# A decoder layer in split fp32: three operand splits of the second MLP product, and the sums of the first norm, moved in the hand-written order

## The chip, the cores and the metric

One core of a Trainium2 chip runs one launch of the whole step. The metric is device time in microseconds (us), the median of the runs shown. The engines are PE (TensorE, matmuls), DVE (VectorE), ACT (ScalarE), POOL (GpSimd) and SP (SyncE, which here only issues DMAs).

## What is computed

One inference step of a one-layer hybrid decoder over 1104 tokens (16 meta, 1024 prompt, 64 new ones), D_MODEL 1024, D_FF 4096. Cut to what the change touches:

```python
u = _rmsnorm(h, norm_mix)
z = u @ w_in + b_in                 # pooling, conv, q, k, v and gates come out of z
...
h = h + merged.astype(h.dtype) @ w_out
u2 = _rmsnorm(h, norm_mlp)
h = h + jnp.square(jax.nn.relu(u2 @ w_up)) @ w_down
```

## The kernel before, in words

**Numbers.** Every fp32 operand of a product is split into a high part (ACT writes it, `hi = Copy(x)`) and a low part (DVE writes it, `lo = x - hi`), and three matmuls, hi·hi, hi·lo and lo·hi, make one product. A split is therefore one ACT and one DVE instruction, in `split` (L155 to L157) for activations and in `Weights.split_to` (L93, L94) for weights. In `split_to` the DVE half is put off until `flush`, and the raw weight comes by a DMA (L64) into one of two buffers.

**Order.** The whole program runs under a manual schedule: each engine takes its instructions in the order in which the code issues them, and waits where an operand or a buffer is not ready. `slot()` issues the DMA stores put off so far, and takes steps from a list.

**Head.** The first five tiles of `w_in` (NHEAD) meet the tokens in three chunks of 416, 320 and 368 (CH). `proj_mm(ti, ci)` is the product of weight tile `ti` with chunk `ci` on PE, 24 matmuls, into a PSUM bank; `proj_chunk` reads that bank on DVE (`un`, L903, times the norm factor `rb`) and ACT. PSUM has three banks called `pm` and two called `pn` for these products, taken in turn, so that product (0,1), tile 0 with chunk 1, writes the bank in which product (0,0) stood, and has to wait for its `un`. `norm1(ci)` is the norm of chunk 1 or 2 as a list of steps: steps 0 and 1 square the chunk on ACT and add it up on DVE (`sq`, L304, L306); step 2 (`s1`) sums over the partitions on PE (L260), makes the factor on DVE and ACT (L246 to L251) and spreads it into three diagonal blocks on DVE (`diag`, L266); step 3 (`s2`) multiplies these with ones on PE, which broadcasts the factor (`px`, L271). In the code `n1` is chunk 1 and `n2` chunk 2, so `n1[2]` is the sum of chunk 1 and `n2[3]` the broadcast of chunk 2.

**First MLP product.** Sixteen pairs of tiles of `w_up` (NPAIR), each by seven block products (`product`, a Strassen-Winograd scheme), i = 0 to 6. Product 6 adds onto the bank of products 0, 2 and 4, so it must wait until DVE has read product 4 out of it (`cb`, L1614). `op_steps` squares the result and makes the seven combinations that the second product takes; they go to memory (`opB..`, `opT..`).

**Second MLP product.** Seven products n = 0 to 6, each of four row pairs `mp` with two half-products `hf` of 48 matmuls (`dprod`); half-product 0 takes the operand pages 0 to 3, half-product 1 the pages 4 to 7. An operand page (n, q) is loaded by `op_load` (L1547, tile `ld`, one of five `page2` buffers) and split by `op_split` into `oph` and `opl`. Pages 0 to 6 of product n = 0 are loaded and split beside the seven products of the last pair; page 7 comes straight from the last steps, without memory. The weights of half-products 1 and 2 are loaded (`W.load_to(3)`) beside product 4 of the last pair. In the split loop and in `dprod`'s loop the order is what is written there, nothing else.

Of the kernel before, what the change touches and what calls it, by code (L numbers as in the profile page):

```python
# [114 lines left out]
def hybrid_trunk_kernel(ctx, tc, I, O):  # L115
# [16 lines left out]
    def pmain():  # L132
        W.tick()
        if wide:
            wide[0] += 1
            if wide[0] % 5 > 2:
                return psum.tile([P, 512], F32, name="pn", tag="qk", bufs=2)
        return psum.tile([P, 512], F32, name="pm", tag="pm", bufs=3)
# [9 lines left out]
    def mm3(ps, wh, wl, pairs, first=True, last=True):  # L148
        n = len(pairs)
        for i, (k, (xh, xl)) in enumerate(pairs):  # L150
            PE.matmul(ps, lhsT=wh[k], rhs=xh, start=first and i == 0, stop=False)  # L151
            PE.matmul(ps, lhsT=wh[k], rhs=xl, start=False, stop=False)  # L152
            PE.matmul(ps, lhsT=wl[k], rhs=xh, start=False, stop=last and i == n - 1)  # L153
# [689 lines left out]
    def sview(t, off, n):  # L843
        return t[:, off:off + 8 * n].rearrange("p (s t) -> p s t", s=8)
# [34 lines left out]
    def proj_mm(ti, ci):  # L879
        kind, j = TILES[ti]  # L880
        wh, wl = wts[ti][:2]
        a, c = CH[ci]
        if kind in "qz" and ci == 0:
            a = NM
        ps = pmain()
        mm3(ps[:, :c - a], wh, wl, [(k, (Uh[k][:, a:c], Ul[k][:, a:c])) for k in range(8)])
        return ps

    def proj_chunk(ti, ci, ps=None):
        kind, j = TILES[ti]  # L890
        t = wts[ti][2]
        if ps is None:
            ps = proj_mm(ti, ci)
        e, es = t.get("e"), t.get("s")
        b = bin_[:, ti:ti + 1]
        a, c = CH[ci]
        if kind in "qz" and ci == 0:
            a = NM
        w = c - a
        pp = min(c, S0) - a  # L900
        if ci < 2 and ti < NHEAD:
            un = apool.tile([P, 416], F32, name="un", tag="zs", bufs=2)
            V.tensor_tensor(un[:, :w], ps[:, :w], rb[:, a:c], ALU.mult)  # L903
            ps = un
        if kind == "g":
            A.activation(sig[j - 4][:, a:c], ps[:, :w], AF.Identity if ti < NHEAD else AF.Sigmoid,
                         bias=b)
        elif kind == "c" and ti < NHEAD:
            A.activation(e[:, 14 + a:14 + a + pp], ps[:, :pp], AF.Identity, bias=b)
            if ci == 2:  # L910
                A.activation(es[:, :, 30:], sview(ps, pp, 8), AF.Identity, bias=b)
        elif kind == "c":
            V.scalar_tensor_tensor(e[:, 14 + a:14 + a + pp], ps[:, :pp], b,
                                   sig[j][:, a:a + pp], ALU.add, ALU.mult)
            if ci == 2:
                V.scalar_tensor_tensor(es[:, :, 30:], sview(ps, pp, 8), b,
                                       sview(sig[j], S0, 8), ALU.add, ALU.mult)
        elif kind == "a":
            A.activation(e[:, a:a + pp], ps[:, :pp], AF.Identity, bias=b)
            if ci == 2:  # L920
                A.activation(es[:, :, 15:], sview(ps, pp, 8), AF.Identity, bias=b)
        elif kind in "kv":
            A.activation(e[:, a:c], ps[:, :w], AF.Identity, bias=b)
        elif kind == "q":
            A.activation(e[:, a - NM:c - NM], ps[:, :w], AF.Identity, bias=b)
        else:
            z = apool.tile([P, 416], F32, name="zs", tag="zs", bufs=2)
            A.activation(z[:, :w], ps[:, :w], AF.Identity, bias=b)
            store(gD[j][:, a - NM:c - NM], z[:, :w])
# [136 lines left out]
    b0_ = [proj_mm(0, 0)]  # L1066
# [27 lines left out]
    n2 = norm1(2)  # L1094
    proj_open(4)
    b0_.append(proj_mm(4, 0))
    n1[2]()
    n2[0]()
    n2[1]()
    proj_chunk(3, 0, b0_[3])  # L1100
    b1_ = [proj_mm(0, 1)]
    proj_chunk(4, 0, b0_[4])
    b1_.append(proj_mm(1, 1))
    n1[3]()
    n2[2]()
    b1_.append(proj_mm(2, 1))
    proj_chunk(0, 1, b1_[0])
    proj_chunk(1, 1, b1_[1])
    n2[3]()
# [434 lines left out]
    def op_load(n, q):  # L1544
        if n < NPROD:
            ld[n, q] = page2("ld")
            SP.dma_start(ld[n, q][:, :L], opD[DORD[n][1], q])  # L1547

    def op_split(n, q):
        if n < NPROD:  # L1550
            t = ld.pop((n, q))
            h, l = BD[n, q] = page("oph", F32R), page("opl", F32R)
            split(h[:, :L], l[:, :L], t[:, :L])
# [27 lines left out]
    for s in range(7 * NPAIR):  # L1581
        j, i = divmod(s, 7)
        if j and i < 4:
            steps[i]()
        if i == 0:
            sums = down_sums(j)
        if i in sums:
            sums[i]()
        if i == 0:
            ca, cb, s15, u2 = page("ca"), page("cb"), page("s15"), page("u2")  # L1590
            bk = [wide_tile(), None, None]
        elif i == 1:
            bk[1] = wide_tile()
        elif i == 5:
            bk[2] = wide_tile()
        if s + 3 < 7 * NPAIR:
            prep(s + 3)
        if j == NPAIR - 1 and i == 0:
            W.load_to(1)
            op_load(0, 0)  # L1600
            op_load(0, 1)
        if j + 1 < NPAIR and 2 <= i < 6:
            sum_pair(j + 1, i - 2)
        product(bk[(0, 1, 0, 1, 0, 2, 0)[i]], s, i, i in (0, 1, 5))
        if i == 0:
            A.activation(two(s15), view(bk[0]), AF.Copy)
        elif i == 1:
            A.activation(two(s15, HL), view(bk[1]), AF.Copy)
        elif i == 2:
            A.activation(two(u2), view(bk[0]), AF.Copy)  # L1610
        elif i == 3:
            V.tensor_tensor(two(ca, HL), view(bk[1]), two(u2), ALU.add)
        elif i == 4:
            V.tensor_tensor(two(cb, HL), view(bk[0]), two(s15, HL), ALU.add)  # L1614
            if j + 2 < NPAIR:
                load_pair(j + 2)
        elif i == 5:
            V.tensor_tensor(two(ca), view(bk[2]), two(s15), ALU.add)
        else:
            A.activation(two(cb), view(bk[0]), AF.Copy)  # L1620
            square(ca)
            steps = op_steps(j, ca, cb)
        if j == NPAIR - 1:
            for n in range(2):
                BC.pop((BX[i], n))
            if i < 5:
                op_split(0, i)
                op_load(0, i + 2)
            elif i == 5:
                op_split(0, 5)  # L1630
                op_split(0, 6)
                op_load(1, 0)
                op_load(1, 1)
            if i == 1:
                W.split_to(1)
                W.flush()
            elif i == 4:
                W.load_to(3)
            elif i == 5:
                W.split_to(2)  # L1640
                W.flush()
        slot()
# [134 lines left out]
    for n in range(NPROD - 1):  # L1777
        for mp in range(4):
            if n == 0:
                H[2 * mp], H[2 * mp + 1] = page("h"), page("h")  # L1780
            b = wide_tile()
            for hf in range(2):
                i = 8 * n + 2 * mp + hf
                WD[n, mp, hf] = W.get(i)
                W.split_to(i + 2)
                W.flush()
                q = 2 * mp + hf
                op_split(n + 1, q)
                if q < 6:
                    op_load(n + 1, q + 2)  # L1790
                elif n + 2 < NPROD:
                    op_load(n + 2, q - 6)
                if 3 <= n < 6 and hf:
                    if n != 5:
                        residual_load(2 * mp + (n == 3), HI)
                    if n != 3:
                        residual_load(2 * mp + (n == 5), LO)
                if n == NPROD - 2 and q == 7:
                    W.load_to(i + 4)
                dprod(n, mp, hf, b, TWO)  # L1800
                WD.pop((n, mp, hf))
                slot(3 if n == 4 and hf == 0 else 1)
            evict(n, mp, b)
            if n == 3:
                attq.extend(done(2 * mp + 1, HI))
            elif n == 4:
                attq.extend(done(2 * mp, HI))
                attq.append(lambda m=2 * mp: residual(m, LO))
            elif n == 5:
                attq.append(lambda m=2 * mp + 1: residual(m, LO))  # L1810


    n = NPROD - 1
# [4 lines left out]
    for e, (a, c) in enumerate(ENDS):  # L1818
        w = c - a
        q = None  # L1820
        for mp in range(4):
            b = wide_tile()
            for hf in range(2):
                i = 8 * n + 2 * mp + hf
# [11 lines left out]
            q = page("fsq")  # L1836
# [139 lines left out]
```

## Time and profile before

| | us |
|---|---|
| median of 3 runs (1661.28 to 1661.79) | 1661.78 |
| the profiled execution, its own time | 1662.0 |
| its span, first to last instruction | 1660.1 |
| PE busy in it (99% of the span) | 1642.7 |
| DVE busy (68%) | 1134.5 |
| ACT busy (45%) | 750.5 |

The span is what the trace covers; 1.9 us of the execution's own time lie around it. PE is busy nearly all the time, so a row matters where PE waits, where it runs at the lower of its two clocks, and where another engine's queue decides when PE may go on. In a timeline row the first number is the start in us from the span's start, the second the length from the first start to the last end of the merged instructions; `[idle before <-releaser]` stands behind a row before which its engine waited. Matmuls overlap, so a matmul's length is more than the distance to the next.

### The profile page before, as it was taken

The numbers are of one execution on the slowest core, as the hardware profiler recorded it, in microseconds if no ns is written. First come the engines' busy times: TensorE is split into PE (matmuls) and PEld (weight loads), VectorE is DVE, ScalarE is ACT, GpSimd is POOL, SyncE is SP. The second block draws the span as 40 slices with busy tenths as digits, with TensorE's granted clock in tenths as the row PEclk, the third lists the DMA queues.
The fourth block names the chain that finished last, engine by engine and source line by source line (L and its number), as shares of the span: only waits on it lengthen the run. The fifth ranks groups of instructions, "written<-read, shape, count | busy, mean of one in ns | idle before, by whom it ended". The sixth has DMA issues, their size and how long they took to land.

```text
span 1660.1 us, 28943 instructions
## 1 busy us (share of the span) xinstructions
PE 1642.7 (99%) x11568; PEld 1618.2 (97%) x11568; DVE 1134.5 (68%) x2120; ACT 750.5 (45%) x1428; POOL 5.8 (0%) x14
## 2 busy tenths in 40 slices
PE   9999999999999999999999999999999999999997
PEld 8999999999999999999999999999999999999997
DVE  7786767867776666455584687777777844457674
ACT  6537667467675342364243343233332533333341
POOL 0000000000000000000000000000000000000000
PEclk9999999999999999999999999999999999999998
DMA  6051221231225353344253447777776955556652
GB/s 207 15 110 52 71 79 42 68 77 41 81 63 173 97 197 113 104 184 146 80 172 124 152 162 242 244 237 246 243 241 227 323 194 184 183 184 222 204 173 85
DMA packets 132123, 250.78 MB, mean 151 GB/s; under 512 B 33459, under 2 KB 64148, under 8 KB 131988
## 3 DMA queue, kind: packets, MB, share of 16 engines
q1 hardware_dynamic: 131428, 248.45, 46.2%
q8 instruction: 91, 1.49, 0.4%
q10 hardware_dynamic: 560, 0.48, 0.1%
q14 instruction: 44, 0.36, 0.1%
HBM read 168.52 MB, written 80.36 MB: 150 GB/s over the span
## 4 chain that ended last, share of the span: by engine, by line
PE 95%; DVE 2%; ACT 1%; DMA 1%; issue 0%; SPq 0%; DVEq 0%; ACTq 0%
PE pm L151 13%; PE pm L153 13%; PE pm L152 13%; PE m L1663 7%; PE m L1665 7%; PE m L1667 7%; PE m L1470 6%; PE m L1473 6%; PE m L1472 6%; PE pn L151 3%; PE pn L153 3%; PE pn L152 3%; PE px L634 2%; PE px L622 2%; PE qk L581 2%; PE px L271 1%
## 5 line engine op out<-in xcount | busy, mean ns | idle before, releaser
L151 PE MATMUL pm<-uh,whi 128*128 128x320 f32 (+3 forms) x1008 | 338.5, 336 | 0.6 <-ACT uh L342 0.5
L153 PE MATMUL pm<-uh,wlo 128*128 128x320 f32 (+3 forms) x1008 | 333.1, 330 | 0.0
L152 PE MATMUL pm<-ul,whi 128*128 128x320 f32 (+3 forms) x1008 | 332.2, 330 | 0.6 <-DVE ul L343 0.6
L1663 PE MATMUL m<-oph,whi 128*128 128x272 f32 (+2 forms) x896 | 258.5, 289 | 0.0
L1665 PE MATMUL m<-opl,whi 128*128 128x272 f32 (+2 forms) x896 | 258.0, 288 | 0.0
L1667 PE MATMUL m<-oph,wlo 128*128 128x272 f32 (+2 forms) x896 | 257.8, 288 | 0.0
L93 ACT ACTIVATE whi<-wraw 128x1024 fp32r<-128x1024 f32 (+1 forms) x127 | 130.0, 1025 | 205.6 <-PE m L1665 138.3
L94 DVE TENSOR_TENSOR wlo<-wraw,whi 128x1024 fp32r<-128x1024 f32 (+1 forms) x127 | 150.6, 1187 | 98.3 <-ACT whi L93 98.3
L151 PEld LDWEIGHTS pm<-uh,whi 128*128 128x128 f32 x1008 | 190.8, 189 | 2.6 <-ACT uh L342 1.3
L152 PEld LDWEIGHTS pm<-ul,whi 128*128 128x128 f32 x1008 | 191.3, 190 | 1.9 <-DVE ul L343 1.5
L153 PEld LDWEIGHTS pm<-uh,wlo 128*128 128x128 f32 x1008 | 190.3, 189 | 0.4
L1665 PEld LDWEIGHTS m<-opl,whi 128*128 128x128 f32 x896 | 168.8, 188 | 0.0
L1663 PEld LDWEIGHTS m<-oph,whi 128*128 128x128 f32 x896 | 168.6, 188 | 0.0
L1667 PEld LDWEIGHTS m<-oph,wlo 128*128 128x128 f32 x896 | 168.5, 188 | 0.0
L456 DVE SCALAR_TENSOR_TENSOR y<-ext,vec,y 128x1024 f32<-128x1024 f32 x120 | 152.5, 1271 | 0.0
L1470 PE MATMUL m<-bch,wlo 128*128 128x272 f32 x448 | 129.2, 288 | 2.0 <-DVE cb L1614 2.0
L1470 PE MATMUL m<-bch,whi 128*128 128x272 f32 x448 | 129.3, 289 | 0.6 <-DVE h L1409 0.6
L1473 PE MATMUL m<-bch,whi 128*128 128x272 f32 x448 | 128.9, 288 | 0.0
L1473 PE MATMUL m<-bch,wlo 128*128 128x272 f32 x448 | 128.8, 288 | 0.0
L1472 PE MATMUL m<-bcl,whi 128*128 128x272 f32 x448 | 128.7, 287 | 0.0
L1472 PE MATMUL m<-bcl,wlo 128*128 128x272 f32 x448 | 128.7, 287 | 0.0
L1470 PEld LDWEIGHTS m<-bch,wlo 128*128 128x128 f32 x448 | 84.2, 188 | 2.2 <-issue 2.2
(364 smaller groups left out, 3418.1 us busy)
## 6 DMA issues: line engine op xcount, KB each, us to landing
wraw<-w_in SPq DMA_DIRECT2D x46, 512.0 KB, 3.9
opT<-d SPq DMA_DIRECT2D x64, 272.0 KB, 3.0
ld<-opT SPq DMA_DIRECT2D x32, 544.0 KB, 4.6
wd<-w_down SPq DMA_DIRECT2D x32, 512.0 KB, 5.8
sumD<-wd SPq DMA_DIRECT2D x32, 512.0 KB, 4.3
wraw<-sumD SPq DMA_DIRECT2D x32, 512.0 KB, 3.6
gt<-gD SPq DMA_DIRECT2D x24, 544.0 KB, 4.7
ld<-opB SPq DMA_DIRECT2D x23, 544.0 KB, 4.7
```

The source lines that it names most:

```text
L93: self.nc.scalar.activation(hi, r, AF.Copy)
L94: self.late.append(lambda lo=lo, r=r, hi=hi: self.nc.vector.tensor_tensor(lo, r, hi.bitcast(F32), ALU.subtract))
L151: PE.matmul(ps, lhsT=wh[k], rhs=xh, start=first and i == 0, stop=False)
L152: PE.matmul(ps, lhsT=wh[k], rhs=xl, start=False, stop=False)
L153: PE.matmul(ps, lhsT=wl[k], rhs=xh, start=False, stop=last and i == n - 1)
L456: V.scalar_tensor_tensor(y[:, :NP], e[:, k:k + NP], w, y[:, :NP], ALU.mult, ALU.add)
L1470: PE.matmul(ps, lhsT=wh, rhs=xh, start=first and k == 0, stop=False, skip_group_check=True)
L1472: PE.matmul(ps, lhsT=wh, rhs=xl, start=False, stop=False, skip_group_check=True)
L1473: PE.matmul(ps, lhsT=wl, rhs=xh, start=False, stop=k == 3, skip_group_check=True)
L1663: PE.matmul(ps, lhsT=wh[:, w], rhs=xh[:, r], start=k == 0, stop=False, skip_group_check=True)
L1665: PE.matmul(ps, lhsT=wh[:, w], rhs=xl[:, r], start=False, stop=False, skip_group_check=True)
L1667: PE.matmul(ps, lhsT=wl[:, w], rhs=xh[:, r], start=False, stop=k == 15, skip_group_check=True)
```

## The change

In the head, the read-out of product (3,0) and the product (0,1) now stand ahead of the sum of chunk 1 (`n1[2]`), and product (2,1) stands ahead of the broadcast of chunk 1 and the sum of chunk 2, which are then followed by the broadcast of chunk 2. In the last pair of the first MLP product, operand pages 4, 5 and 6 are no longer split beside products 4 and 5; they are split in half-product 0 of the second MLP product, behind the last pair's steps, and the load of page (1,1) stands behind the split of page 4. The load of page (1,0) stays.

```diff
@@ -1094,16 +1094,16 @@
     n2 = norm1(2)
     proj_open(4)
     b0_.append(proj_mm(4, 0))
+    proj_chunk(3, 0, b0_[3])
+    b1_ = [proj_mm(0, 1)]
     n1[2]()
     n2[0]()
     n2[1]()
-    proj_chunk(3, 0, b0_[3])
-    b1_ = [proj_mm(0, 1)]
     proj_chunk(4, 0, b0_[4])
     b1_.append(proj_mm(1, 1))
+    b1_.append(proj_mm(2, 1))
     n1[3]()
     n2[2]()
-    b1_.append(proj_mm(2, 1))
     proj_chunk(0, 1, b1_[0])
     proj_chunk(1, 1, b1_[1])
     n2[3]()
@@ -1623,14 +1623,12 @@
         if j == NPAIR - 1:
             for n in range(2):
                 BC.pop((BX[i], n))
+            if i < 4:
+                op_split(0, i)
             if i < 5:
-                op_split(0, i)
                 op_load(0, i + 2)
             elif i == 5:
-                op_split(0, 5)
-                op_split(0, 6)
                 op_load(1, 0)
-                op_load(1, 1)
             if i == 1:
                 W.split_to(1)
                 W.flush()
@@ -1785,6 +1783,11 @@
                 W.split_to(i + 2)
                 W.flush()
                 q = 2 * mp + hf
+                if n == q == 0:
+                    op_split(0, 4)
+                    op_load(1, 1)
+                    op_split(0, 5)
+                    op_split(0, 6)
                 op_split(n + 1, q)
                 if q < 6:
                     op_load(n + 1, q + 2)
```

PE in the head, from the end of product (4,0) to product (0,1) and at the two later places where a sum or a broadcast moved (`st` are the sums, `px` the broadcasts, `pm` and `pn` the products; - is before, + is after):

```order
 L153 MATMUL pm<-uh_116,wlo 128x400
-L260 MATMUL st_468<-ones,sq 128x1 x3
 L151 MATMUL pm<-uh_109,whi 128x320
...
 L153 MATMUL pm<-uh_116,wlo 128x320
-L271 MATMUL px<-diag,ones 128x128 x3
-L260 MATMUL st_562<-ones,sq 128x1 x3
 L151 MATMUL pn<-uh_109,whi 128x320
...
 L153 MATMUL pn<-uh_116,wlo 128x320
+L271 MATMUL px<-diag,ones 128x128 x3
+L260 MATMUL st_587<-ones,sq 128x1 x3
 L271 MATMUL px<-diag,ones 128x128 x3
 L151 MATMUL pn<-uh_109,whi 128x320
```

The sum of chunk 2 (`st_562` before, `st_587` after) had product (2,1) between itself and its broadcast; now the broadcast is the next instruction.

DVE before, from the read-out of product 4 of the last pair to the first split of operand n = 1 (`ld_13912`, `ld_13950` and the next are pages 4, 5 and 6, `cb` and `ca` the read-outs of products 4 and 5, `L94` the weight of half-product 1, `L1477` the first of the last steps):

```order
L1614 TENSOR_TENSOR cb_13787<-m2_13790,s15_13788 128x544
L157 TENSOR_TENSOR opl_13981<-ld_13912,oph_13980 128x1088
L999 TENSOR_TENSOR wd_13782<-wd_13782 128x512
L1618 TENSOR_TENSOR ca_13786<-m2_13991,s15_13788 128x544
L157 TENSOR_TENSOR opl_14018<-ld_13950,oph_14017 128x1088
L157 TENSOR_TENSOR opl_14022<-ld_13984,oph_14021 128x1088
L94 TENSOR_TENSOR wlo_14030<-wraw_13986,whi_14029 128x1024
L1477 SCALAR_TENSOR_TENSOR ca_13786<-ca_13786 128x1088
```

DVE after, at the same place:

```order
L1614 TENSOR_TENSOR cb_13787<-m2_13790,s15_13788 128x544
L999 TENSOR_TENSOR wd_13782<-wd_13782 128x512
L1618 TENSOR_TENSOR ca_13786<-m2_13987,s15_13788 128x544
L94 TENSOR_TENSOR wlo_14016<-wraw_13982,whi_14015 128x1024
L1477 SCALAR_TENSOR_TENSOR ca_13786<-ca_13786 128x1088
...
L1517 TENSOR_TENSOR d34_14052<-cb_13787,d12_14050 128x544
L157 TENSOR_TENSOR opl_14060<-ld_13912,oph_14059 128x1088
L157 TENSOR_TENSOR opl_14066<-ld_13950,oph_14065 128x1088
L157 TENSOR_TENSOR opl_14070<-ld_13980,oph_14069 128x1088
```

The three splits left their places behind L1614 and L1618 and now follow the last of the pair's steps (L1517); what stands ahead of L1614 is the same row for row.

## Rows read from the trace of the kernel before

**Rows 1.** waits of PE over the whole span: for whom, us, times, longest

```profile
PE m L1470 <- DVE cb L1614: 2.0, 1, 2.0
PE px L271 <- DVE diag L266: 1.7, 1, 1.7
...
PE st L260 <- DVE sq L306: 1.1, 1, 1.1
```

**Rows 2.** timeline of PE in the head: start, length, operation, idle before

```profile
33.20 0.35 PE L153 MATMUL pm<-uh,wlo 128*128 128x400 f32 x1
34.68 0.80 PE L260 MATMUL st<-ones,sq 128*128 128x1 f32 x6 [1.13 <-DVE sq L306]
35.34 0.39 PE L151 MATMUL pm<-uh,whi 128*128 128x320 f32 x1
...
44.70 0.73 PE L260 MATMUL st<-ones,sq 128*128 128x1 f32 x6
45.29 0.39 PE L151 MATMUL pn<-uh,whi 128*128 128x320 f32 x1
...
48.90 0.83 PE L271 MATMUL px<-diag,ones 128*128 128x128 f32 x6
```

**Rows 3.** timeline of DVE in the head, the same columns

```profile
30.46 4.07 DVE L306 TENSOR_TENSOR sq<-sq 128x320 f32<-128x320 f32 x7 [1.60 <-ACT sq L304]
34.45 1.08 DVE L903 TENSOR_TENSOR un<-pm,rb 128x416 f32<-128x416 f32 x2
...
38.53 4.41 DVE L306 TENSOR_TENSOR sq<-sq 128x368 f32<-128x368 f32 x7
...
45.47 0.16 DVE L246 TENSOR_SCALAR st<-st 128x3 f32<-128x3 f32 x1 [1.54 <-PE st L260]
...
46.70 0.68 DVE L266 TENSOR_SCALAR diag<-ident,st 128x128 f32<-128x128 f32 x3
```

**Rows 4.** three stretches: busy us of PE, PEld, DVE, ACT, POOL; clock; DMA

```profile
35.70:39.12 3.42, 3.42 (x15) 3.42 (x14) 2.44 (x10) 3.30 (x10) 0.00 (x0) 0.51 0.01 2
...
1302.95:1306.06 3.11, 3.07 (x24) 3.10 (x25) 3.11 (x4) 1.55 (x2) 0.00 (x0) 1.00 1.03 422
1650.20:1653.00 2.80, 1.19 (x4) 0.93 (x4) 1.25 (x7) 1.00 (x3) 0.00 (x0) 0.51 0.00 0
```

**Rows 5.** timeline of PE from the last pair into the second MLP product

```profile
1302.99 0.36 PE L1470 MATMUL m<-bch,wlo 128*128 128x272 f32 x1 [2.02 <-DVE cb L1614]
...
1306.06 0.29 PE L1663 MATMUL m<-oph,whi 128*128 128x272 f32 x1
...
1312.18 0.29 PE L1665 MATMUL m<-opl,whi 128*128 128x272 f32 x1
```

**Rows 6.** timeline of DVE at the same place

```profile
1289.27 1.29 DVE L157 TENSOR_TENSOR opl<-ld,oph 128x1088 fp32r<-128x1088 f32 x1 [3.07 <-ACT oph L156]
...
1302.13 0.72 DVE L1614 TENSOR_TENSOR cb<-m,s 128x544 f32<-128x544 f32 x1
1302.76 1.28 DVE L157 TENSOR_TENSOR opl<-ld,oph 128x1088 fp32r<-128x1088 f32 x1
...
1304.57 0.72 DVE L1618 TENSOR_TENSOR ca<-m,s 128x544 f32<-128x544 f32 x1
1305.20 2.48 DVE L157 TENSOR_TENSOR opl<-ld,oph 128x1088 fp32r<-128x1088 f32 x2
1307.60 1.22 DVE L94 TENSOR_TENSOR wlo<-wraw,whi 128x1024 fp32r<-128x1024 f32 x1
...
1315.26 1.29 DVE L157 TENSOR_TENSOR opl<-ld,oph 128x1088 fp32r<-128x1088 f32 x1
```

**Rows 7.** timeline of ACT, the hi half of the second weight

```profile
1306.16 1.06 ACT L93 ACTIVATE whi<-wraw 128x1024 fp32r<-128x1024 f32 x1
```

**Rows 8.** timeline of SP's queue, the issue of that weight's load

```profile
1298.24 1.90 SPq L64 DMA_DIRECT2D wraw<-w_down  x2
```

**Rows 9.** line 64 alone from 1298.2 to 1298.7: landing of that load

```profile
DMA to landing us min/median/max: 7.8/7.8/7.8
```

## The prediction

> **What bounds the kernel now.** I read the shares of busy time first: PE is busy for 99% of the span, so only three things count, a wait of PE, a stretch at its lower clock, and another queue's place that decides when PE goes on. Second, the list of PE's waits [rows 1]: three long ones, two of which are at the places that the change touches. The 2.0 us on L1614 stand in the last pair of the first MLP product, the 1.1 us on L306 stand in the head; the 1.7 us on `diag` are at the end of the kernel and are not touched, but they are the price of a sum with its broadcast right behind it. [...]
>
> **Head, product (0,1) ahead of the sum of chunk 1.** The squares of chunk 1 end on DVE at 30.46 + 4.07 = 34.53, and PE's sums start 0.15 later [rows 2, 3]. Product (0,1) does not need them, but it needs the bank of product (0,0), and the `un` that empties this bank is the next instruction on DVE: two of them from 34.45, 1.08 in all, so the first ends at about 35.0 [rows 3]. With the 0.14 us that PE takes to follow DVE elsewhere (1302.13 + 0.72 to 1302.99) [rows 5, 6], the product starts at 35.1 instead of 35.34: a gain of 0.2 only. PE's wait doesn't go, it changes its cause, and grows from 1.13 to about 1.6 us, since the sums (34.68 to 35.34, 0.66 us) are no longer done in it. They now cost 0.66 us behind the product, where nothing is waiting to be covered. Sum so far: +0.5.
>
> **Head, sum and broadcast of chunk 2 side by side.** Before, product (2,1) ran from 45.29 to 48.90 between the sums and the broadcast [rows 2]; DVE needed from 45.47 to 46.70 + 0.68 = 47.38 for the factor [rows 3], which was hidden. Now the broadcast is PE's next instruction behind the sums, so this chain lies open: 45.29 to 47.38 with 0.14 to follow is 2.2 us to the last block, less what of the broadcast runs meanwhile, and the same pattern at the end of the kernel waited 1.7 us [rows 1]. I take 1.7, with 1.4 and 2.2 as ends. What else moved is covered: DVE now sits behind the later sums of chunk 1 (until about 41 us), then needs 1.9 us for that factor and 4.4 us for the squares of chunk 2 [rows 3], to about 47.4; PE, after 35.1, one product with 1.7 us of low clock in it, the sums and two more products of 3.6 us [rows 2], gets to the sums of chunk 2 at about 48.9, so 1.5 us of cover is left. Head in all: 0.5 + 1.7 = **+2.2 us**.
>
> **Last pair, what the moved splits free.** The wait of 2.02 us ends with L1614, and DVE is without idle time from 1289.27 until then [rows 6]; the order shows that no row ahead of L1614 changed. So this wait stays: **0**. Behind L1614, L1618 comes one split earlier: 1304.57 − 1.20 = 1303.4, done at 1304.1 (1.20 us is the distance of two splits, from 1305.20 to 1307.60) [rows 6]. Nobody waits for it.
>
> **Last pair, the hole.** Next on DVE is now L94, the low part of the weight of half-product 1. Its high half began on ACT at 1306.16 and took 1.06 [rows 7]; the raw weight was issued at 1298.24 and took 7.8 us to land, to 1306.04 [rows 8, 9]. Nothing ahead of that issue on SP's queue is changed. So L94 starts at about 1307.2 instead of 1307.60, and DVE stands idle from 1304.1 to 1307.2, the 3.1 us that two of the moved splits filled before, while all three splits now lie behind it.
>
> **Half-product 0, the splits.** From L94 to the split behind the pair's last step DVE took 1315.26 − 1307.60 = 7.66 us [rows 6]. Page 4 is now the one that stands there: 1307.2 + 7.66 = 1314.9, done 1.29 later at 1316.15, seen by PE at 1316.3. PE wants it as the low part of the first matmul triple of half-product 1, which ran at 1312.18 [rows 5]. That is a wait of **+4.1 us**, a new one. Pages 5 and 6 follow at 1.20 us each and PE takes 1.5 us for a page (a quarter of 1306.06 to 1312.06), so they cost nothing. The high parts are not the limit: ACT has no work but these splits behind the steps. The load of (1,1) on SP's queue now waits for the split of page 4, and the loads and stores behind it, the weight of half-product 3 among them, go out some 5 us later than before; PE is 4 us later too, and this weight isn't wanted until two half-products on, so I cost it at nothing; without that cover it would be up to 1 us. Ends for the wait: 0.9, if the weight is there by 1304.1 (1307.2 − 1304.1 = 3.1 less), and 4.5, if L94 comes no earlier than before.
>
> **Clock.** The head's low stretch around 33 to 35 us is 0.2 us shorter and keeps its fall, I think. Two new stretches come in which PE does hardly any column: the broadcast of chunk 1, the sums, the wait and the next broadcast, nearly 4 us, and the 4.1 us before page 4. Both are longer than the 1.13 us with its sums that were followed by a fall, and than the 2.02 us that were not [rows 2, 4, 5]; the 1.7 us wait at the end of the kernel [rows 1] also lies in a stretch at 0.51 [rows 4]. Each fall costs up to 1.7 us, none below zero. I take one and a half of them, 2.5 us, with 0 and 3.4 as ends. [...]
>
> **Sum.** The profiled execution took 1662.0 us, 0.2 above the median. 1662.0 + 2.2 + 4.1 + 2.5 = 1670.8, less 0.2: **1670.6 us** (about +0.5%).
>
> **The rivals.** (a) Both waits, and no fall beyond the old one: 1661.8 + 6.3 = 1668.1. For it: the 2.02 us row. Against: both gaps are twice as long. If the old fall in the head went too, 1666.4. (b) More falls than two, since a gap of about 2 us is followed by one in the head and by none at L1614 [rows 4, 5], so the latter, or the sums before the first MLP product, may go the other way once they come later. A fall at L1614 is partly covered, as PE then comes later to page 4. 1672 to 1674. (c) The hole closes: a transfer under less load brings the weight by 1304.1, the new wait is 0.9 with no fall behind it, and the head costs 2.2 with or without one: 1664.9 to 1666.6. Against it: the load is issued under the same DMA traffic, 7.8 us. (d) Faster: the engines are not held to the written order and take what is ready past a waiting instruction. Then the splits do free DVE for L1614 (−2.0), product (0,1) fills PE's wait (−1.1) and the fall goes (−1.7): 1661.8 − 4.8 = 1657.0. It decides at L1614, if it starts before 1302.1 relative to product 5. Against it: DVE idled 3.07 us behind `oph` at 1289.27 with ready work queued behind [rows 6].
>
> **How the numbers follow.** My case, both waits with one or two falls, 0.63; (a) 0.13; (b) 0.11; (c) 0.09; (d) 0.04. The range that leaves out (d), the lower half of (c) and the upper part of (b) is **1666.0 to 1673.3**. A measurement of this kernel can tell 0.2%, 3.3 us, from no change: faster than 1658.5 only in (d), 0.04; within it the low end of (c) and mixtures of (c) and (d), 0.07; slower 0.89.
>
> **What would show it.** Right: in the list of PE's waits, a new one on `opl` L157 of about 4 us at the start of half-product 1, one on `diag` L266 of 1.7 us in the head beside the one at the end, 2.0 us on L1614 as before, the head's wait on `sq` replaced by one on `un` L903 of 1.6 us; on DVE an idle time of 3 us before L94, put down to ACT `whi`; granted clock near 0.5 for 3.4 us behind one or both new waits. Wrong: L1614's wait gone, no wait on L157, or product (0,1) starting at 33.4 right behind product (4,0).

## The result, and the profile after

The changed kernel takes 1670.95 us, the median of 4 runs (1668.18 to 1672.66), against 1661.78 for the kernel before (1661.28 to 1662.65). The ratio is 1.0053, with a 95% interval of 1.0036 to 1.007: slower by about 9 us, as forecast (1670.6). The profiled execution took 1671.75, with a span of 1668.8; it is this one whose rows follow.

First the waits of PE in the kernel after (for whom, what released it, us in all, times, longest), to be held against [rows 1]. Behind the split loop of the last pair its line numbers are 2 lower than those of before, so L1663 is the L1665 of [rows 5]:

```profile
PE m L1663 <- DVE opl L157: 4.1, 1, 4.1
PE px L271 <- DVE diag L266: 3.4, 2, 1.7
PE m L1470 <- DVE cb L1614: 2.2, 1, 2.2
PE pm L151 <- DVE un L903: 1.6, 1, 1.6
```

All four were forecast: 4.1 on a split at the start of half-product 1, a second `diag` of 1.7, L1614 as it was (2.0 before), and 1.6 on `un` in the place of 1.1 on `sq`.

The head, on PE and then on DVE (start, length, operation, idle before and its releaser). Before: [rows 2, 3].

```profile
34.96 0.35 PE L153 MATMUL pm<-uh,wlo 128*128 128x400 f32 x1
...
36.88 0.41 PE L151 MATMUL pm<-uh,whi 128*128 128x320 f32 x1 [1.58 <-DVE un L903]
...
40.51 0.73 PE L260 MATMUL st<-ones,sq 128*128 128x1 f32 x6
41.10 0.39 PE L151 MATMUL pm<-uh,whi 128*128 128x320 f32 x1
...
48.92 0.73 PE L260 MATMUL st<-ones,sq 128*128 128x1 f32 x6
51.35 0.91 PE L271 MATMUL px<-diag,ones 128*128 128x128 f32 x6 [1.70 <-DVE diag L266]
```

```profile
36.24 1.08 DVE L903 TENSOR_TENSOR un<-pm,rb 128x416 f32<-128x416 f32 x2
...
46.80 1.19 DVE L306 TENSOR_TENSOR sq<-sq 128x368 f32<-128x368 f32 x2 [0.58 <-ACT sq L304]
...
49.69 0.16 DVE L246 TENSOR_SCALAR st<-st 128x3 f32<-128x3 f32 x1 [1.21 <-PE st L260]
...
50.92 0.68 DVE L266 TENSOR_SCALAR diag<-ident,st 128x128 f32<-128x128 f32 x3
```

The reader sees three things. Product (0,1) doesn't start behind product (4,0) (35.3) but when the first `un` is done, 36.24 and about 0.54. The sums of chunk 1 take 0.59 us of PE's own time behind it (40.51 to 41.10). And the factor of chunk 2, on DVE from 49.69 to 51.60, is what PE waits for, with nothing between the sums and the broadcast. From the last matmul of product (4,0) to the broadcast of chunk 2 it was 48.90 − 33.20 = 15.70 us, and is 51.35 − 34.96 = 16.39. Only 0.7 more, since the stretch at a granted clock of 0.51 that followed the wait on `sq` [rows 4] (such a stretch, about 0.5 against 1.00 around it, is called a fall of the clock or the lower level from here on) is gone in this execution:

```profile
35.70:39.12 3.42, 2.24 (x15) 2.24 (x16) 2.65 (x6) 2.13 (x4) 0.00 (x0) 1.00 0.00 0
1319.20:1322.70 3.50, 3.05 (x13) 3.05 (x14) 3.50 (x4) 0.00 (x0) 0.00 (x0) 0.51 0.62 177
```

These are two stretches of the kernel after, with busy us of PE, PEld, DVE, ACT and POOL, granted clock (1.00 in the head, 0.51 behind the wait on `opl`), DMA share and GB/s. With the 1.7 us of the missing fall, an estimate from [rows 4] (3.42 × 0.49), the waits and sums of the head cost 2.4 us more.

The last pair and half-products 0 and 1, on PE, DVE, ACT and SP's queue. Before: [rows 5 to 8].

```profile
1306.19 0.36 PE L1470 MATMUL m<-bch,wlo 128*128 128x272 f32 x1 [2.18 <-DVE cb L1614]
...
1319.65 0.60 PE L1663 MATMUL m<-opl,whi 128*128 128x272 f32 x1 [4.06 <-DVE opl L157]
```

```profile
1305.33 0.71 DVE L1614 TENSOR_TENSOR cb<-m,s 128x544 f32<-128x544 f32 x1
...
1306.56 0.71 DVE L1618 TENSOR_TENSOR ca<-m,s 128x544 f32<-128x544 f32 x1
1310.66 1.23 DVE L94 TENSOR_TENSOR wlo<-wraw,whi 128x1024 fp32r<-128x1024 f32 x1 [3.38 <-ACT whi L93]
...
1317.68 0.72 DVE L1517 TENSOR_TENSOR d<-cb,d 128x544 f32<-128x544 f32 x1
1318.32 4.89 DVE L157 TENSOR_TENSOR opl<-ld,oph 128x1088 fp32r<-128x1088 f32 x4
```

```profile
1309.56 1.06 ACT L93 ACTIVATE whi<-wraw 128x1024 fp32r<-128x1024 f32 x1 [9.85 <-DMA wraw<-w_down]
```

```profile
1301.82 1.51 SPq L64 DMA_DIRECT2D wraw<-w_down  x2
...
1319.63 1.53 SPq L1547 DMA_DIRECT2D ld<-opT  x2
```

The landing of that load, from line 64 alone, 1301.5 to 1302.5 us ([rows 9] before):

```profile
DMA to landing us min/median/max: 7.6/7.6/7.6
```

L1614 ends the wait of product 6 as before. DVE then stands idle for 3.38 us (the hole) until the weight, whose load was issued at 1301.82, has landed and its high half is written. L94 and the pair's steps follow, and the split of page 4 is done at 1318.32 + 1.22 = 1319.5; PE goes on at 1319.65. The load of page (1,1), which needs the buffer that this split empties, goes out on SP's queue in the same moment, and the loads behind it follow.

### The profile page after: what moved, and what is told of

It reads as the page before. It is cut to its first block, busy times and chain, and to the rows that moved or that the text cites. A ratio compares the mean times of both kernels' runs of the same rounds, so it can differ in the third digit from the quotient of the medians.

```text
span 1668.8 us, 28936 instructions
## 1 busy us (share of the span) xinstructions
PE 1644.6 (99%) x11568; PEld 1619.4 (97%) x11568; DVE 1134.5 (68%) x2120; ACT 750.4 (45%) x1428; POOL 5.8 (0%) x14
## 4 chain that ended last, share of the span: by engine, by line
PE 94%; DVE 2%; ACT 1%; DMA 1%; issue 0%; SPq 0%; DVEq 0%; ACTq 0%
PE pm L151 13%; PE pm L152 12%; PE pm L153 12%; PE m L1663 7%; PE m L1661 7%; PE m L1665 7%; PE m L1470 6%; PE m L1473 6%; PE m L1472 6%; PE pn L151 3%; PE pn L153 3%; PE pn L152 3%; PE px L634 2%; PE px L622 2%; PE qk L581 2%; PE px L271 1%
## 5 line engine op out<-in xcount | busy, mean ns | idle before, releaser
L1663 PE MATMUL m<-opl,whi 128*128 128x272 f32 (+2 forms) x896 | 258.6, 289 | 4.1 <-DVE opl L157 4.1
L1665 PE MATMUL m<-oph,wlo 128*128 128x272 f32 (+2 forms) x896 | 258.3, 288 | 0.0
L94 DVE TENSOR_TENSOR wlo<-wraw,whi 128x1024 fp32r<-128x1024 f32 (+1 forms) x127 | 150.6, 1186 | 103.6 <-ACT whi L93 103.5
L1663 PEld LDWEIGHTS m<-opl,whi 128*128 128x128 f32 x896 | 169.4, 189 | 4.3 <-DVE opl L157 4.3
L1665 PEld LDWEIGHTS m<-oph,wlo 128*128 128x128 f32 x896 | 169.2, 189 | 0.0
```

What stands on the lines that cost most here:

```text
L94: self.late.append(lambda lo=lo, r=r, hi=hi: self.nc.vector.tensor_tensor(lo, r, hi.bitcast(F32), ALU.subtract))
L1663: PE.matmul(ps, lhsT=wh[:, w], rhs=xl[:, r], start=False, stop=False, skip_group_check=True)
L1665: PE.matmul(ps, lhsT=wl[:, w], rhs=xh[:, r], start=False, stop=k == 15, skip_group_check=True)
```

## What one time of this kernel is made of

An execution lists its span and mean granted clock. By the time alone a wait can't be told from a stretch at the lower level, so I split each span in two, as an estimate: span × (1 − clock), the part given to the lower level, and span × clock, the rest. The clock is given to 0.001, which is 1.7 us, so only means over executions are used; the first part also holds the last microseconds of the kernel, in which PE has nothing to do (a clock of 0.50 from 1653 us on in the trace of before), so only differences count.

| kernel | executions | median us | ratio, 95% | to the clock | rest | rest to before |
|---|---|---|---|---|---|---|
| before | 48 | 1661.67 and 1662.55 | | 7.1 | 1653.2 | |
| after | 5 | 1670.95 (of the first 4) | 1.0036 to 1.007 | 10.0 | 1659.1 | +5.9 |
| head alone | 10 | 1665.89 | 1.0009 to 1.0028 | 8.5 | 1655.2 | +2.0 |
| tail alone | 6 | 1668.62 | 1.0026 to 1.0049 | 9.2 | 1656.9 | +3.7 |
| after, (2,1) back | 4 | 1672.89 | 1.0034 to 1.0076 | 11.3 | 1659.1 | +5.9 |
| splits ahead of the steps | 10 | 1663.71 | 1.0001 to 1.002 | 7.0 | 1654.6 | +1.4 |
| tail, weight early | 10 | 1663.73 | 0.9999 to 1.0017 | 6.5 | 1655.1 | +1.9 |
| squares early | 11 | 1659.91 | 0.9977 to 0.9995 | 7.1 | 1651.1 | −2.1 |
| hole filled | 11 | 1660.26 | 0.9976 to 0.9994 | 6.2 | 1651.9 | −1.2 |
| both of these | 5 | 1656.91 | 0.9951 to 0.9978 | 5.6 | 1649.7 | −3.5 |

The 48 executions of before are 21 beside the first four experiments and 27 beside the next four, hence two medians; ratios are to those of the same chip. The two groups give 6.7 and 7.3 us to the clock and leave 1653.2 and 1653.1, so the table takes them together. The fifth execution of after is a later one with a second trace. The standard error is 0.1 to 0.4 us for the means of the rest and 0.3 to 1.9 for those of the clock. Held against the waits in the traces, the rest is off by about 1 us in two rows that no timeline here explains: squares early (−2.1 for a wait of 1.1) and weight early (1.8 less than the tail alone, for 2.9 less wait). The 48 executions spread from 1659.93 to 1665.3, and the clock goes with it: 16 of them have 0.997 and took 1659.93 to 1661.59, the three at 0.994 and 0.993 took over 1665.

## The experiments

**The head's part of the change alone.**

```diff
+    proj_chunk(3, 0, b0_[3])
+    b1_ = [proj_mm(0, 1)]
     n1[2]()
...
-    proj_chunk(3, 0, b0_[3])
-    b1_ = [proj_mm(0, 1)]
...
+    b1_.append(proj_mm(2, 1))
     n1[3]()
     n2[2]()
-    b1_.append(proj_mm(2, 1))
```

> Only the head of the change, the last pair and half-product 0 as before. My account: PE waits 1.6 us for un L903 where it waited 1.13 us for the squares, the sums of chunk 1 cost 0.66 us behind the product, and the broadcast of chunk 2 waits 1.7 us for its factor right behind the sums: +2.2 us with the clock as it was, 1664.0, and 1662.3 if the fall of the clock behind 35 us goes, as it did in the trace of the changed kernel. No wait on opl L157, 2.0 us on L1614. Rival (the head is what makes the tail late): nearly all of the 9 us, 1669 or more. Rival (the head's wait is simply gone): 1659 to 1661.

1665.89, ratio 1.0019: 2 us above the upper end expected. The waits are those forecast: `diag` 3.4 in two, `un` 1.6, nothing on `opl`. The trace has a stretch of 3.4 us at the lower level (0.50) behind the wait on `diag` and another near 992 us, where nothing was moved. Without the clock the head costs 2.0 us, near the 2.2 forecast; what was missed is the clock, 8.5 us against 6.7 in the 21 executions of before beside it.

**The tail's part alone** (the second and third piece of the change, the head as before).

> Only the three splits moved, the head as before. My account: a new wait of 4.1 us on opl L157 at the start of half-product 1, an idle time of DVE of about 3 us before L94, the wait on L1614 still 2.0 us, one fall of the clock behind the new wait (up to 1.7 us): 1666 to 1667.6. Rival (the tail costs only because the head shifted it): 1662. Rival (the moved splits free L1614): its wait shrinks, the time below 1664.

```profile
PE m L1663 <- DVE opl L157: 3.9, 1, 3.9
```

1668.62, ratio 1.0037, 1 us above the upper end expected; PE waited 3.9 on `opl`, and a fall follows (a mean clock of 0.62 from 1316.0 to 1320.5 us). Both parts cost time by themselves, and 0.19% and 0.37% add up to what the whole change cost, 0.53%: neither paid for the other.

**Product (2,1) back between the sums and the broadcast of chunk 2.**

```diff
-    b1_.append(proj_mm(2, 1))
     n1[3]()
     n2[2]()
+    b1_.append(proj_mm(2, 1))
```

> The changed kernel with product (2,1) put back between the sums and the broadcast of chunk 2; the sums of chunk 1 stay behind product (0,1). If the price of the head is the order of this product alone, the 1.7 us wait on diag goes and the time is 1669.2. My account: the squares of chunk 2 stand behind the late sums of chunk 1 on DVE and end near 48 us, while PE is at the sums of chunk 2 near 45.4 us, so a wait of about 2.7 us on sq L306 takes its place: 1 us slower than the changed kernel, 1672, up to the clock.

The waits of PE in this kernel:

```profile
PE m L1663 <- DVE opl L157: 4.2, 1, 4.2
...
PE st L260 <- DVE sq L306: 2.0, 1, 2.0
PE px L271 <- DVE diag L266: 1.7, 1, 1.7
```

The `diag` in the head is gone (the 1.7 left is that at the end), and 2.0 us on the squares of chunk 2 have come, since PE now asks for them one product earlier. The wait is 0.7 less than expected: in this trace the squares end at 47.2 us, not near 48, and PE is ready for them at 45.2. The product was the cover of either one or the other. 1672.89, not better than after.

**The splits ahead of the last pair's steps**, in the place of half-product 0, the head as before.

```diff
         slot()
+    op_split(0, 4)
+    op_load(1, 1)
+    op_split(0, 5)
+    op_split(0, 6)
     steps[0]()
...
-                if n == q == 0:
-                    op_split(0, 4)
-                    op_load(1, 1)
-                    op_split(0, 5)
-                    op_split(0, 6)
```

> The head as before; pages 4, 5 and 6 split behind product 6 of the last pair, but ahead of the last pair's steps instead of behind them; the load of (1,1) goes with them. My account: the place behind the steps is what makes the wait. DVE still idles 3 us before L94, but page 4 is done near 1310.9, before PE wants it at 1312.2, pages 5 and 6 in time too, and the last steps have until 1316.6 for page 7: no wait on opl, 2.0 us on L1614, 1661.8 within 0.7. Rival (the splits are late because the pages or their loads come late, wherever they stand): a wait of 2 us or more on opl stays, 1664 or more.

The wait on `opl` went, but the time didn't come back (1663.71). PE at the only new wait, and DVE from the hole to there:

```profile
1318.46 0.39 PE L1669 MATMUL m<-oph,wlo 128*128 128x272 f32 x1 [1.96 <-DVE wlo L94]
```

```profile
1305.54 1.22 DVE L94 TENSOR_TENSOR wlo<-wraw,whi 128x1024 fp32r<-128x1024 f32 x1 [3.45 <-ACT whi L93]
...
1307.88 3.69 DVE L157 TENSOR_TENSOR opl<-ld,oph 128x1088 fp32r<-128x1088 f32 x3
...
1315.99 1.28 DVE L157 TENSOR_TENSOR opl<-ld,oph 128x1088 fp32r<-128x1088 f32 x1
1317.19 1.22 DVE L94 TENSOR_TENSOR wlo<-wraw,whi 128x1024 fp32r<-128x1024 f32 x1
```

I had missed this. The three splits, 3.69 us, were done in the hole before; now DVE idles there for 3.45 us and does them later, and whatever stands last in its queue comes late. With the splits ahead of the steps that is the weight of half-product 2, 2.0 us. So moving the splits ahead of the steps takes back some 2 of the 4 us, and with this order the other 2 return at the next thing that is late. That no order behind the hole does better isn't shown. The split of page (1,0) stands right ahead of that L94 and takes 1.20 us (1315.99 to 1317.19); with the weight split first, as in the experiment on L1614 below, about 0.8 of the 2.0 would be left, by an estimate from these rows. No run tried it.

**The tail with the hole closed**: the weight of half-product 1 kept in pages of its own and loaded two products earlier, all else as in the tail alone.

```diff
-                                  n == mp == hf == 0 or
+                                  n == mp == 0 or
...
                 op_load(0, i + 2)
+                if i == 2:
+                    W.load_to(2)
```

> The moved splits as in the changed kernel, behind the last steps, the head as before; the weight of half-product 1 is loaded two products earlier and lies in pages, so that DVE need not wait for it. My account: the idle time of 3 us before L94 goes, everything behind it on DVE is 3.1 us earlier, and of the wait of 3.9 to 4.1 us on opl L157 about 0.9 is left: 1662.6, against 1668.6 with the moved splits alone. Rival (the place behind the steps makes the whole wait, the hole is idle time that costs nothing): the wait stays near 4 us, 1667 or more.

```profile
1305.19 1.22 DVE L94 TENSOR_TENSOR wlo<-wraw,whi 128x1024 fp32r<-128x1024 f32 x1
...
1310.20 0.73 DVE L157 TENSOR_TENSOR opl<-ca,oph 128x544 fp32r<-128x544 f32 x1 [2.60 <-ACT oph L156]
```

```profile
PE m L1665 <- DVE opl L157: 1.0, 1, 1.0
```

L94 follows L1618 without idle time, and the wait on `opl` is 1.0 instead of 3.9, as forecast (0.9). The 2.60 us that DVE idles later are on ACT, which waits for product 6; PE ran that product at the lower level in this trace (from 1304.9 to 1307.9 us its matmuls start 0.23 us apart, ahead of the wait and from 1308.05 on 0.12). 1663.73, ratio 1.0008, against 1.0037 with the hole; of the difference 1.8 us are in the rest, and the others in the clock, as no fall follows the wait of 1.0. The two remedies overlap: by the waits the other place takes back 2 of the 4 us by itself and the closed hole 3, so the 4 us can't be dealt out between the two causes.

**The squares of chunk 1 earlier**, in the kernel before: the squares for which the sums of chunk 1 wait are moved forward.

```diff
+    n1 = norm1(1)
+    n1[0]()
     hs[3]()
     load_x(2)
-    n1 = norm1(1)
-    n1[0]()
     n1[1]()
```

> The kernel before with one edit in the head: the first four squares of chunk 1 stand ahead of the broadcast of chunk 0 on ACT and DVE, which were idle there, so that the sums of chunk 1 need not wait. My account of the head (the wait of 1.1 us on the squares and the clock that falls behind it in some executions): the wait on sq L306 goes, 1.1 us, and with it a fall of up to 1.7 us where there was one: 1659.5 within 1. Rival (the wait moves on to un L903 or to the next sums): 1661.7, with a new wait of the same size in the list of PE.

```profile
33.05 0.80 PE L260 MATMUL st<-ones,sq 128*128 128x1 f32 x6
```

The sums start without a wait (1.13 us in [rows 2]), `sq` is gone from the list of PE's waits and no other came. 1659.91, ratio 0.9986, as forecast, but none of it comes from the clock (7.1 us, as in before).

**L1614 earlier**, in the kernel before: the splits of pages 3 and 4 behind the read-outs of products 4 and 5, two sums of the low weight (`wd`, L999) behind both, and the weight of half-product 2 split ahead of page (1,0).

```diff
-        if i in sums:
+        if i in sums and not (j == NPAIR - 1 and i in (4, 5)):
             sums[i]()
...
-            if i < 5:
+            if i < 3:
                 op_split(0, i)
+            if i == 4:
+                op_split(0, 3)
+            if i < 5:
                 op_load(0, i + 2)
             elif i == 5:
+                sums[4]()
+                sums[5]()
+                op_split(0, 4)
                 op_split(0, 5)
...
                 q = 2 * mp + hf
+                if n == q == 0:
+                    W.split_to(3)
+                    W.flush()
                 op_split(n + 1, q)
```

> The opposite of the change at the last pair: the split of page 3 and two sums of w_down (L999) are taken from ahead of L1614 and put with pages 4 to 6 into DVE's time before the weight lands, and the weight of half-product 2 is split ahead of page (1,0). My account (DVE's queue ahead of L1614 sets PE's wait, the time before the weight lands is free): L1614 starts 1.8 us earlier, its wait falls from 2.0 to about 0.3, nothing new: 1660.0 within 0.8. Rival (what is taken from there comes back as a wait on opl or on the weight L94 of half-product 2): 1661.7, with such a wait of 1 to 2 us.

```profile
1302.23 0.37 PE L1470 MATMUL m<-bch,wlo 128*128 128x272 f32 x1 [0.29 <-DVE cb L1614]
```

```profile
1301.37 0.71 DVE L1614 TENSOR_TENSOR cb<-m,s 128x544 f32<-128x544 f32 x1
1302.00 1.28 DVE L157 TENSOR_TENSOR opl<-ld,oph 128x1088 fp32r<-128x1088 f32 x1
1303.20 0.72 DVE L1618 TENSOR_TENSOR ca<-m,s 128x544 f32<-128x544 f32 x1
1303.84 1.41 DVE L999 TENSOR_TENSOR wd<-wd 128x512 f32<-128x512 f32 x2
1305.16 3.69 DVE L157 TENSOR_TENSOR opl<-ld,oph 128x1088 fp32r<-128x1088 f32 x3
1308.77 1.22 DVE L94 TENSOR_TENSOR wlo<-wraw,whi 128x1024 fp32r<-128x1024 f32 x1
```

L1614 comes earlier when work that stood ahead of it goes, here a split and a sum, and the three other splits with the two sums fill the hole, so that L94 waits for nothing. The wait of 2.0 us is 0.3, and no other has come. 1660.26, ratio 0.9985, as forecast.

**Both of these together.**

> Both edits, the early squares and the filled hole. If the two places are independent, their gains add: 2.8 us of waits less and the fall of the clock in the head, 1658.2 within 1. Rival (a gain in the head is given back at the last pair because the loads there come no earlier): the same as the better one alone, about 1659.5.

1656.91, ratio 0.9964 (0.9951 to 0.9978): faster than before by some 6 us, where 3.5 were forecast. Without the clock it is 3.5, and the two places alone gave 2.1 and 1.2, so those gains add up; the remainder is the clock, 5.6 us against 7.1, over five executions only. After, by its own ratio, is 0.9% slower than this.

**Do falls of the clock belong to the waits?** The first traces had them in different places, so three kernels were profiled once more, unchanged.

> The changed kernel once more, unchanged, for a second trace of it. Both theories expect the same waits of PE as in its first trace (4.1 us on opl L157, two of 1.7 on diag L266, 2.2 on L1614, 1.6 on un L903). Theory that a fall of the clock belongs to the wait ahead of it: the same stretches at the lower level as in the first trace, 3.4 us behind the wait on opl, none between 30 and 55 us, none near 990 us, and a time within 1 us of 1671.75. Rival, that most falls come or stay out by chance from execution to execution: the one behind the wait on opl is there again, but the first stretch (8 to 16 us in the first trace) lasts half as long, or another stretch turns up at 36, 50 or 990 us; the time then differs by 1.7 us for each.

> The kernel before once more, unchanged, for a second trace of it. Same waits in both theories. If the falls belong to the waits: one of 3.4 us at 36 us behind the wait on sq, one at 8 to 12 us, one at the end, as in its first trace, and nowhere else. If they come by chance: the one at 36 us is absent or another turns up (50 or 990 us), 1.7 us of time for each.

> The head's part of the change alone once more (product (0,1) ahead of the sum of chunk 1, product (2,1) ahead of the sum of chunk 2), unchanged, for a second trace of it. Same waits in both theories. If the falls belong to the waits: stretches at the lower level at 50 us, behind the new wait on diag, and near 992 us, as in its first trace. If they come by chance: one or both are absent, or another is there, 1.7 us of time for each.

The waits at the places of the change repeat to 0.2 us: after, for one, has 4.0 on `opl`, 1.7 twice on `diag`, 2.0 on L1614, 1.5 on `un`. The falls don't. Three stretches of the second trace of after (1674.73 us), then one of the second of before (1662.96), which begins with the sums behind the wait on `sq`:

```profile
52.00:55.40 3.40, 3.40 (x16) 3.40 (x15) 3.33 (x8) 2.38 (x5) 0.00 (x0) 0.56 0.00 0
993.80:997.20 3.40, 3.40 (x19) 3.40 (x20) 3.33 (x14) 0.00 (x0) 0.00 (x0) 0.60 0.67 250
1322.00:1325.50 3.50, 3.15 (x14) 3.16 (x15) 3.50 (x4) 0.00 (x0) 0.00 (x0) 0.53 0.65 184
```

```profile
36.92:40.34 3.42, 3.42 (x25) 3.42 (x26) 2.33 (x9) 2.90 (x7) 0.00 (x0) 1.00 0.01 2
```

After got a fall behind the head's `diag` and one at 994 us that its first trace hadn't, each 1.7 us of time by the same estimate. In the second trace of before the same wait of 1.1 us on `sq` stands in the head and the clock behind it is 1.00, where the first had 0.51 [rows 4]; its time is no shorter, because its stretch at the start is twice as long (0.50 to 0.54 from 9.35 to 16.15 us, in the first 0.51 from 8.40 to 11.80). The second trace of the head alone (1664.26 us, the first 1666.74) has neither of the two falls of its first, at 50 and 992 us, and another one instead, behind the wait on L1614:

```profile
1304.00:1307.40 3.40, 3.40 (x17) 3.40 (x17) 3.40 (x5) 1.62 (x3) 0.00 (x0) 0.52 1.02 418
```

So the theory that a fall belongs to the wait ahead of it is out, but for the wait of 4 us. All 13 traces, read in steps of 0.85 us:

| what PE did ahead | traces that have it | of them with a fall behind it |
|---|---|---|
| 4 us of wait on `opl` | 4 | 4 (one of them twice as long) |
| wait on `sq` of 1.1 us, then the sums of chunk 1 | 6 | 4 |
| wait on `un` of 1.6 us, no sums | 5 | 0 |
| head of after: sums or broadcast of chunk 2 with a wait of 1.7 or 2.0 | 5 | 3 |
| wait ahead of product 6 of the last pair of 1.8 to 2.2 us | 11 | 2 |
| 18 sums of one column, 2.2 us, no wait (near 990 us) | 13 | 4 |
| start, 8 to 16 us | 13 | 9 (five of them twice as long) |

The falls near 990 us stand right behind the sums of the norm before the first MLP product. In the second trace of after they run from 991.83 us on and the first MLP matmul starts at 993.86:

```profile
991.83 2.17 PE L260 MATMUL px<-ones,sqa 128*128 128x1 f32 x18
```

## Why the prediction was right, step by step

- **Product (0,1) gains next to nothing, since the bank decides.** Right: 1.58 us on `un`, 1.6 forecast.
- **The sums of chunk 1 are no longer covered (+0.66), and the broadcast of chunk 2 waits 1.7.** Right: 0.59 and 1.70. The head was put at +2.2 without the clock; the distance from product (4,0) to that broadcast gives 2.4, and the ten executions of the head alone 2.0.
- **L1614's wait stays.** Right: 2.18 and, in the second trace, 2.0. The wait goes only with work that stood ahead of L1614 (the hole filled: 0.29).
- **The hole.** Right: 3.38 us idle before L94, 3.1 forecast. The row of the weight's landing carried it: the transfer took 7.6 us, 7.8 before.
- **The wait on the split of page 4.** Right: 4.06, forecast 4.1. The tail alone costs 3.7 without the clock by its executions.
- **What the hole has to do with that wait.** The prediction had it at the low end of its range: 0.9 would be left with the weight there by 1304.1, and with the hole closed 1.0 was left. What missed is the later forecast for the splits ahead of the steps (1661.8 within 0.7, measured 1663.71). There I took the 4.1 us as a question of the place alone, and left out that the DVE time lost in the hole, 3.45 us, returns at the next thing that is late: 2.0 us at the weight of half-product 2.
- **The clock, one and a half falls, 2.5 us.** By the executions the whole change gave 10.0 − 7.1 = 2.9 us to the lower level, by the first four alone 9.2 − 7.1 = 2.1, with a standard error of 1.2 and 1.1; the size is borne out no more closely than that. The 1.7 us for one fall, which the forecast used for the head as well, are an estimate from [rows 4], 3.42 × (1 − 0.51), which counts all of the clock that is not granted as lost time. The matmuls' starts show about 1.5: in that stretch of before 14 of 320 columns take 3.59 us (35.72 to 39.31), and 14 behind it, 0.15 us apart, 2.1; in the trace of weight early 16 of 272 columns take 3.54 us (1304.51 to 1308.05) instead of 2.0. And I had the places wrong in the first trace: there the old fall in the head, which I kept, is missing, one fall stands behind `opl`, none behind `diag`, and the stretch at the start is twice as long (3.4 us of time instead of 1.7, at 8 to 16 us; a clock of 0.54 from 8.0 to 14.8, 0.75 in before), which stands ahead of all that the change touches. That this trace's time (1671.75) lies near the forecast is partly chance; the median and the split of the spans are the better witness.
- **The rivals.** (a), no more falls: in all 4 traces with the wait of 4 us a fall stands behind it, yet one of the four executions took 1668.18 with a clock of 0.996, which is the time of (a); it has no trace, so (a) is excluded as the usual case only. (b), more falls, holds in single executions: the second trace of after, with two more, took 1674.73, and one of the two stands behind the sums before the first MLP product, which (b) had named. (c), the hole closes, is excluded by the 3.38 us. (d), engines take ready work past a waiting instruction, is excluded by L1614's wait of 2.18 and by the hole, in which L1477 stood behind L94, though its input had been written by L1618 at 1307.3.

The same kernel shows falls at different places from one execution to the next. Between 8 and 16 us 4 of 13 traces have no stretch at the lower level, 4 have one of 3.4 us, and 5 one twice as long. In the middle of the kernel too, behind waits of 1 to 2 us, a fall comes in some executions and not in others: behind the 1.7 or 2.0 us in the head in 3 of 5, behind the 1.8 to 2.2 us ahead of product 6 in 2 of 11. Only behind the wait of 4 us did one come each time (4 of 4).

Open: what decides whether a fall comes. Near 990 us PE had no wait of more than 0.3 us in the 15 us ahead, only the 18 sums of one column, and a fall came in 4 of 13 traces. So a fall came there without a longer wait, with sums of one column ahead of it. In the head neither did it alone: 0 of 5 behind the wait on `un` without sums, 0 of 7 behind the six sums of chunk 1 without a wait, but 4 of 6 behind the wait on `sq` with its sums. No run varied the sums by themselves.

## What to carry to other kernels

Before work is moved off a queue to let something pass, see whether that something stands behind it or ahead of it: the splits stood behind L1614 and could free nothing (its wait was 2.02 us and is 2.18), and they were the filling of a hole that a late transfer leaves. DVE's waiting time there, filled with useful work before, became idle time once the work was moved behind it (3.38 us), and with the splits ahead of the steps it came back at what was next to be late (2.0 us at the weight of half-product 2), so look for the second-latest item too. In a chain of sum, factor and broadcast, the product between its parts is cover: moved ahead, it must be replaced (here PE waited 1.70 us without it).

## What the runs showed of the hardware

The same kernel's executions on one chip differ by up to 5.4 us (21 of the kernel before, 1659.93 to 1665.3; 27 on another chip, 1660.04 to 1665.13), and the granted clock goes with it (0.997 to 0.993). The falls in these traces lasted 3.4 us or twice that, at a granted clock of about 0.5, by the estimates above 1.5 to 1.7 us of time for each 3.4; behind a wait of 4 us one came each time (4 of 4), behind 1 to 2 us in some executions only (3 of 5 and 2 of 11), and behind 2.2 us of one-column sums, with no wait of more than 0.3 us in the 15 us ahead, in 4 of 13. The executions of before have a standard deviation of 1.5 to 1.8 us, so by an estimate from it ten of them give a mean to about 0.5 us: to tell 2 us from nothing, a kernel has to run ten times or so. A single trace's falls are no property of the kernel. Its waits on other engines at the places of the change are, as they repeated to 0.2 us; the wait on ACT's L342 near the start didn't (0.5 us in one trace of before, 1.4 in the other).
